# Fetching the second output tile's weights before the first's, in every pair of a block-product up-projection

## The chip, the cores and the metric

The kernel runs on one core of one Trainium2 chip. The metric is the time of one execution on the device, in microseconds (us), as the median of several runs. The core has a matrix engine (TensorE, PE in the profile), three engines that work on rows of data (VectorE, DVE; ScalarE, ACT; GpSimd, POOL), and SyncE (SP), which here issues the DMAs. Each engine works through its own queue of instructions in order and waits on semaphores for the others.

## The reference

The program is a small encoder of two layers with width 1024, all in 32-bit floats. Two sequences, a sample of 512 tokens and a prompt of 256, go through the same weights: 768 tokens in all. Layer 0 mixes tokens with an mLSTM, layer 1 with sliding-window attention. After the mixer, each layer has the part in which the change lies, a feed-forward network with a convolution of width 3 along the tokens:

```python
D_FF = 2816
def conv_ffn(h, w_up, conv_w, conv_b, w_down):
    u = h @ w_up                                  # [.., 1024] @ [1024, 2*2816]
    u = lax.conv_general_dilated(u, conv_w[:, None, :], window_strides=(1,),
                                 padding=((1, 1),), ...,
                                 feature_group_count=2 * D_FF) + conv_b
    g = u[..., :D_FF]
    val = u[..., D_FF:]
    return (jax.nn.silu(g) * val) @ w_down
...
x = x + g2 * conv_ffn(h, ffn_w_up[l], ffn_conv_w[l], ffn_conv_b[l], ffn_w_down[l])
```

## The kernel before

**Products in three parts.** TensorE multiplies a rounded 32-bit format (fp32r). To keep the accuracy of 32 bits, each operand is split in a rounded part hi and a remainder lo, and a product is hi·hi + hi·lo + lo·hi: three matmuls. `fp_copy_split` (L218 to L226) makes the two: ScalarE copies and rounds (L222, a CAST in the profile), VectorE subtracts (L223).

**Weights.** `load(u, h)` (L234) fetches one tile of 128 x 1024 floats (512 KB), half h of weight unit u, into one of five buffers named raw, with a DMA that SP issues (L231). All weights use this ring, those of the down-projection too, and the DMAs keep the order of the calls. `split` (L237) makes whi and wlo of a raw tile, with three buffers each.

**Rounds and pairs.** `ffn` (L1117) works through 11 rounds p = 0 to 10 in each layer. A round makes two pairs of output tiles of the up-projection: pair 0 gives 256 rows of the gate g, pair 1 the 256 rows of val that go with them. A pair is one weight unit: its two raw tiles are the weights of its first and of its second 128 rows of output, over all 1024 input channels. After the pairs of round p comes the down-projection of round p-1 (`down`), 96 matmuls on PSUM tiles named pa, with weights from two more raw tiles; L507 adds its results to the residual.

**A pair is a block product with seven multiplications instead of eight** (Strassen's scheme in Winograd's form). The weights are four blocks: A11 and A12 are the halves (512 columns) of the first tile `ra`, A21 and A22 those of the second tile `rb`; the code calls them q[0] to q[3]. The input, 8 x 128 channels by two halves of 384 tokens, is held as the blocks B11, B21, B22 and their combinations T1 to T4, split once per layer. Each of the seven products is `quarters` (L1034 to L1043): 12 matmuls of 128 x 128 by 128 x 384, at lines 1040, 1041 and 1042. The sums of the weight blocks overwrite the raw tiles in place:

- L1053: S1 = A21 + A22, into q[2]. It needs `rb` alone.
- The split of `ra` as fetched (wa) gives the weights of B11 and B21.
- L1055: S2 = S1 - A11 into q[0], after that split has read A11. L1056: S4 = A12 - S2 into q[1].
- L1078: S1 is split into s1h and s1l, one buffer each, for the product with T1.
- L1079: S3 = A22 - S2 into q[2], after S1 was split.
- The split of `ra` as it is now, S2 and S4 (wc), gives the weights of T2 and B22; the split of `rb`, S3 and A22 (wb), those of T3 and T4.

GpSimd makes these sums, but VectorE makes them for both pairs of round 0 and for pair 0 of round 1 (argument `pool_adds`).

**The PSUM banks of a pair.** Four banks are fixed: a takes B11 (later B21 on top of it), e takes T1, b starts as a copy of a and takes T2, d starts as a copy of b and takes T3 and T4; B22 goes on top of b. ScalarE makes these copies: L1086 (a to b), L1089 (e to p5, in SBUF), L1093 (b to d), L1107 (d to u3). T3 cannot start before the copy at L1093, and that copy not before T2's last matmul. The results go to SBUF by L1067 (ScalarE) and, with an addition, by L1112 and its neighbours (VectorE).

**After a pair**, each of its two rows goes through the convolution: L1127 (ScalarE), then two taps on VectorE, L1129 and L1130. A row of the gate goes through the silu (L1163, ScalarE). A row of val is multiplied with the gate's (L1165, GpSimd) and split.

**Round 0** is special: its two pairs are interleaved with the mixer's output projection and the normalisation of the tokens, whose pieces VectorE does too.

**Order of the work.** The order in which Python calls the operations is not the order in which the engines run them. The program is built with `schedule_with_timeline_sim=True`: a planner runs the whole program through a model of the chip's costs and orders each engine's queue by it. Where a tile becomes ready earlier or later in that model, it may order the queues around it differently.

Of the kernel before, what the change touches and what calls it, by code (L numbers as in the profile page):

```python
# [74 lines left out]
def col(t):  # L75

    return t + (GAP if t >= 256 else 0)


def pieces(c0, c1):  # L80

    return [(max(c0, s0), min(c1, s1), q) for q, (s0, s1) in enumerate(SEQS) if max(c0, s0) < min(c1, s1)]
# [55 lines left out]
class Net:  # L138
# [906 lines left out]
    def pair(self, pool, u, bank, rows, early=False, spare=False, pool_adds=True):  # L1045


        nc = self.nc
        r1, r2 = rows
        ra, rb = (self.load(u, h) for h in range(2))  # L1050
        q = [t[:, 512 * i : 512 * (i + 1)] for t in (ra, rb) for i in range(2)]
        tt = (nc.gpsimd if pool_adds else nc.vector).tensor_tensor
        tt(q[2], q[2], q[3], ALU.add)  # L1053
        wa = self.split(ra)
        tt(q[0], q[2], q[0], ALU.subtract)  # L1055
        tt(q[1], q[1], q[0], ALU.subtract)  # L1056
        if spare:
            s1h, s1l = (lambda t: (t[:, 0], t[:, 1]))(self.slab([P, 2, 512], R))
        else:
            s1h = pool.tile([P, 512], R, tag="s1h", name=self.nm("s1h"), bufs=1)  # L1060
            s1l = pool.tile([P, 512], R, tag="s1l", name=self.nm("s1l"), bufs=1)
        yield
        part = lambda w, i: [t[:, 512 * i : 512 * (i + 1)] for t in w]

        def evict(r, o):
            for p0, p1, _ in pieces(0, H):
                nc.scalar.copy(r[:, col(p0) : col(p0) + p1 - p0], o[:, p0:p1])  # L1067

        a = bank(0)
        self.quarters(a, part(wa, 0), self.B11, True)  # L1070
        fork = a
        if early:
            fork = self.tmp([P, H])
            nc.scalar.copy(fork, a)
            self.quarters(a, part(wa, 1), self.B21, False)
            evict(r1, a)
        yield
        self.fp_copy_split(s1h, s1l, q[2])  # L1078
        tt(q[2], q[3], q[0], ALU.subtract)  # L1079
        wc = self.split(ra)  # L1080
        if early:
            yield
        else:
            wb = self.split(rb)
        e, b = bank(1), bank(2)
        nc.scalar.copy(b, fork)  # L1086
        self.quarters(e, (s1h, s1l), self.T1, True)
        p5 = self.tmp([P, H])
        nc.scalar.copy(p5, e)  # L1089
        yield  # L1090
        self.quarters(b, part(wc, 0), self.T2, False)
        d = bank(3)
        nc.scalar.copy(d, b)  # L1093
        if early:
            wb = self.split(rb)
        yield
        p3 = lambda: self.quarters(b, part(wc, 1), self.B22, False)
        if early:
            p3()
            nc.vector.tensor_tensor(r1[:, col(H) :], b, p5, ALU.add)  # L1100
            yield
        else:
            self.quarters(a, part(wa, 1), self.B21, False)
            evict(r1, a)
        self.quarters(d, part(wb, 0), self.T3, False)
        u3 = self.tmp([P, H])
        nc.scalar.copy(u3, d)  # L1107
        yield
        if not early:
            p3()  # L1110
            nc.vector.tensor_tensor(r1[:, col(H) :], b, p5, ALU.add)
        nc.vector.tensor_tensor(r2[:, col(H) :], e, u3, ALU.add)  # L1112
        self.quarters(d, part(wb, 1), self.T4, False)
        evict(r2, d)
# [282 lines left out]
```

## Time and profile before

| | us |
|---|---|
| median of 3 runs | 1946.82 (1946.59 to 1949.53) |
| profiled execution | 1955.06 |
| its span, first to last instruction | 1953.2 |
| TensorE busy in the span | 1851.3 (95%) |
| VectorE busy | 1390.8 (71%) |
| ScalarE busy | 895.8 (46%) |
| GpSimd busy | 555.1 (28%) |

In the profile, a line of a group or of a timeline names the source line (L1053 is line 1053 of the kernel), the engine, the operation, and the tiles written and read. Brackets at the end of a timeline row give the idle time of that engine just before it, and what ended that wait. Matmuls are pipelined: each is listed with 0.34 us or so, but they start 0.175 us apart where nothing holds them up. The mean clock granted to TensorE over the span was 0.979 of full speed; it is lower in some stretches. The feed-forward network of layer 0 lies from about 545 to 1100 us, that of layer 1 from about 1386 to 1920 us; in between its rounds take about 47.6 us each.

### The profile page before, as it was taken

Reading aid. Unit: us, or ns where it says so; the run is one execution under the profiler, and the core shown is the slowest. Engines: PE = TensorE matmul, PEld = TensorE weight load, DVE = VectorE, ACT = ScalarE, POOL = GpSimd, SP = SyncE. Lnnn points to the kernel's source line nnn. Section 1 sums busy time; section 2 is a strip of 40 time slices with the busy share of each in tenths; the row PEclk is TensorE's granted clock in tenths of the full one; section 3 lists DMA queues with packets and bytes.
Section 4 is the critical chain, followed back from the end, with each engine's and each line's share of the span. In section 5 each row is a group of like instructions: output and inputs, shape, how many; then the busy total and the mean of one; then the engine's idle time right before and its main releaser. Section 6 shows DMA issues by size and latency. Waiting matters only on the chain. (4 is left out here: it accounts for less than half of the span.)

```text
span 1953.2 us, 28783 instructions
## 1 busy us (share of the span) xinstructions
PE 1851.3 (95%) x11122; PEld 1673.9 (86%) x11122; DVE 1390.8 (71%) x2261; ACT 895.8 (46%) x1785; POOL 555.1 (28%) x448
## 2 busy tenths in 40 slices
PE   6799999999979999999999999999799999999997
PEld 3686887888978999999999998779789999999997
DVE  4756675684577777777777765775877777777776
ACT  3343433343446444444444555774554444444442
POOL 4203011032213333333331311342123333333323
PEclk8899999999989999999999999999899999999998
DMA  9335445455212222222222221122212222222211
GB/s 341 100 100 188 150 155 198 150 157 169 76 44 76 65 66 65 65 65 65 65 66 87 98 89 49 40 85 76 65 56 65 72 69 66 72 68 65 65 33 66
DMA packets 63381, 181.32 MB, mean 93 GB/s; under 512 B 6071, under 2 KB 23735, under 8 KB 63244
## 3 DMA queue, kind: packets, MB, share of 16 engines
q1 hardware_dynamic: 63244, 179.49, 28.7%
q8 instruction: 87, 1.43, 0.3%
q14 instruction: 50, 0.41, 0.1%
HBM read 173.03 MB, written 6.43 MB: 92 GB/s over the span
## 5 line engine op out<-in xcount | busy, mean ns | idle before, releaser
L222 ACT CAST whi<-raw 128x1024 fp32r<-128x1024 f32 x247 | 258.5, 1047 | 414.0 <-PE pa L216 202.8
L223 DVE TENSOR_TENSOR wlo<-raw,whi 128x1024 fp32r<-128x1024 f32 x247 | 330.5, 1339 | 104.1 <-ACT whi L222 103.5
L216 PE MATMUL pa<-slab,whi 128*128 128x256 f32 (+1 forms) x1472 | 349.1, 335 | 3.7 <-DVE slab L507 2.6
L216 PEld LDWEIGHTS pa<-slab,whi 128*128 128x128 f32 x1472 | 253.4, 191 | 35.3 <-DVE slab L507 9.2
L507 DVE SCALAR_TENSOR_TENSOR slab<-pa,mod,slab 128x256 f32<-128x256 f32 (+1 forms) x368 | 206.9, 591 | 59.2 <-PE pa L216 59.1
L216 PE MATMUL pa<-slab,wlo 128*128 128x256 f32 (+1 forms) x736 | 234.6, 332 | 0.0
L216 PE MATMUL ps<-zh,whi 128*128 128x256 f32 (+2 forms) x688 | 230.1, 338 | 4.6 <-ACT zh L222 2.7
L216 PE MATMUL ps<-zh,wlo 128*128 128x256 f32 (+2 forms) x688 | 229.3, 337 | 2.8 <-DVE wlo L223 2.8
L216 PE MATMUL ps<-zl,whi 128*128 128x256 f32 (+2 forms) x688 | 231.0, 338 | 0.9 <-DVE zl L477 0.7
L1040 PE MATMUL ps<-zh,whi 128*128 128x384 f32 x504 | 173.7, 345 | 20.9 <-ACT ps L1093 18.2
L1041 PE MATMUL ps<-zl,whi 128*128 128x384 f32 x504 | 171.8, 341 | 4.1 <-DVE zl L223 4.1
L1042 PE MATMUL ps<-zh,wlo 128*128 128x384 f32 x504 | 171.5, 340 | 0.0
L216 PEld LDWEIGHTS pa<-slab,wlo 128*128 128x128 f32 x736 | 140.1, 191 | 12.3
L216 PEld LDWEIGHTS ps<-zh,whi 128*128 128x128 f32 x688 | 132.8, 194 | 20.2 <-ACT zh L222 3.5
L1053 POOL TENSOR_TENSOR raw<-raw 128x512 f32<-128x512 f32 x38 | 69.0, 1815 | 284.3 <-DMA raw<-in_w_dram 132.6
L216 PEld LDWEIGHTS ps<-zh,wlo 128*128 128x128 f32 x688 | 133.4, 194 | 14.1 <-DVE wlo L223 3.4
L216 PEld LDWEIGHTS ps<-zl,whi 128*128 128x128 f32 x688 | 133.4, 194 | 12.3 <-issue 1.7
L1130 DVE SCALAR_TENSOR_TENSOR slab<-slab,cstt,slab 128x771 f32<-128x771 f32 x88 | 131.5, 1496 | 1.4
L1165 POOL TENSOR_TENSOR slab<-slab 128x772 f32<-128x772 f32 x44 | 89.5, 2035 | 139.6 <-DVE slab L1130 124.8
L1055 POOL TENSOR_TENSOR raw<-raw,raw 128x512 f32<-128x512 f32 x38 | 49.1, 1291 | 266.5 <-DVE wlo L223 245.8
L1129 DVE SCALAR_TENSOR_TENSOR slab<-slab,cstt,slab 128x771 f32<-128x771 f32 x88 | 103.0, 1172 | 29.8 <-ACT slab L1127 29.8
L1040 PEld LDWEIGHTS ps<-zh,whi 128*128 128x128 f32 x504 | 96.2, 191 | 29.9 <-ACT ps L1093 24.0
(261 smaller groups left out, 4220.1 us busy)
## 6 DMA issues: line engine op xcount, KB each, us to landing
raw<-in_w_dram SPq DMA_DIRECT2D x202, 512.0 KB, 3.7
raw<-in_adaln_w_dram SPq DMA_DIRECT2D x84, 512.0 KB, 4.3
slab<-in_x_dram SPq DMA_DIRECT2D x12, 512.0 KB, 9.1
slab<-in_adaln_w_dram SPq DMA_DIRECT2D x12, 512.0 KB, 10.2
slab<-mrows SPq DMA_DIRECT2D x8, 384.0 KB, 4.8
xs<-slab SPq DMA_DIRECT2D x6, 512.0 KB, 2.9
bt<-brow SPq DMA_DIRECT2D x16, 192.0 KB, 3.2
slab<-xs SPq DMA_DIRECT2D x6, 512.0 KB, 9.3
```

Source lines behind the costliest of these rows:

```text
L216: self.nc.tensor.matmul(out, lhsT, rhs, start=start, stop=stop)
L222: nc.scalar.copy(hi, src)
L223: nc.vector.tensor_tensor(lo, src, hi.bitcast(F32), ALU.subtract)
L507: self.nc.vector.scalar_tensor_tensor(x, o, self.mod[l][:, gc + c, q : q + 1], x, ALU.mult, ALU.add)
L1040: mm(o, wh[:, k], hi[k], start=start and k == 0, stop=False, skip_group_check=True)
L1041: mm(o, wh[:, k], lo[k], start=False, stop=False, skip_group_check=True)
L1042: mm(o, wl[:, k], hi[k], start=False, stop=k == 3, skip_group_check=True)
L1053: tt(q[2], q[2], q[3], ALU.add)
L1055: tt(q[0], q[2], q[0], ALU.subtract)
L1129: stt(y[:, 1:], u[:, :-1], w(0), y[:, 1:], ALU.mult, ALU.add)
L1130: stt(y[:, :-1], u[:, 1:], w(2), y[:, :-1], ALU.mult, ALU.add)
L1165: nc.gpsimd.tensor_tensor(y, y, yrow[:, j], ALU.mult)
```

## The change

In each pair the two calls of `load` are made in the other order: the DMA of the second tile `rb` is now issued first, that of the first tile `ra` second. Names, sums, splits and products stay as they are. The lines after the changed one read the same tiles as before.

```diff
     def pair(self, pool, u, bank, rows, early=False, spare=False, pool_adds=True):
...
         nc = self.nc
         r1, r2 = rows
-        ra, rb = (self.load(u, h) for h in range(2))
+        rb, ra = (self.load(u, h) for h in (1, 0))
         q = [t[:, 512 * i : 512 * (i + 1)] for t in (ra, rb) for i in range(2)]
         tt = (nc.gpsimd if pool_adds else nc.vector).tensor_tensor
         tt(q[2], q[2], q[3], ALU.add)
```

It holds for all 44 pairs, in both layers, those of round 0 too. The planner builds the queues anew for the changed program.

## The prediction

> **What bounds the kernel now.** I read the page first, then the waits of the stretches in which the changed lines run, then the timeline of one pair of output tiles, engine by engine.
>
> ```profile
> PE 1851.3 (95%) x11122; PEld 1673.9 (86%) x11122; DVE 1390.8 (71%) x2261; ACT 895.8 (46%) x1785; POOL 555.1 (28%) x448
> ```
>
> TensorE is busy for 1851.3 of 1953.2 us. The change adds and removes no matmul, so only the 102 us in which TensorE stands still, and the clock it gets after standing still, can move. The list of waits over the whole span has two links of one chain:
>
> ```profile
> ACT s1h L222 <- POOL raw L1053: 53.3, 18, 3.5
> ...
> PE ps L1040 <- ACT ps L1093: 18.4, 19, 3.2
> ```
>
> Eighteen times the cast of S1 (s1h) waits on ScalarE for POOL's sum at L1053, and about as often (19) TensorE waits for the copy at L1093: 18.4 us in all. How they hang together is seen in one pair, the second pair of a round p from 3 to 9; here the one around 711 us. The columns are start, duration, engine, line, operation, tiles, and in brackets the idle time before and what ended it.
>
> ```profile
> 700.66 0.33 SPq L231 DMA_DIRECT2D raw<-in_w_dram  x1
> ...
> 709.90 0.33 SPq L231 DMA_DIRECT2D raw<-in_w_dram  x1
> ```
> ```profile
> 702.95 1.29 POOL L1055 TENSOR_TENSOR raw<-raw,raw 128x512 f32<-128x512 f32 x1 [13.59 <-DVE wlo L223]
> 704.31 1.29 POOL L1056 TENSOR_TENSOR raw<-raw 128x512 f32<-128x512 f32 x1
> 705.56 2.01 POOL L1079 TENSOR_TENSOR raw<-raw,raw 128x512 f32<-128x512 f32 x1
> 713.77 1.28 POOL L1053 TENSOR_TENSOR raw<-raw 128x512 f32<-128x512 f32 x1 [6.20 <-DMA raw<-in_w_dram]
> ```
> ```profile
> 709.24 1.03 ACT L222 CAST whi<-raw 128x1024 fp32r<-128x1024 f32 x1
> 710.17 0.53 ACT L1067 COPY slab<-ps 128x128 f32<-128x128 f32 x2
> 710.74 1.04 ACT L1127 ACTIVATE slab<-slab,cstt 128x772 f32<-128x772 f32 x1
> 711.68 0.46 ACT L1089 COPY nt<-ps 128x384 f32<-128x384 f32 x1
> 715.08 0.62 ACT L222 CAST s1h<-raw 128x512 fp32r<-128x512 f32 x1 [2.95 <-POOL raw L1053]
> 715.61 0.47 ACT L1093 COPY ps<-ps 128x384 f32<-128x384 f32 x1
> 716.02 0.84 ACT L1163 ACTIVATE slab<-slab 128x772 f32<-128x772 f32 x1
> ```
> ```profile
> 714.72 0.34 PE L1040 MATMUL ps<-yh,whi 128*128 128x384 f32 x1
> 714.89 0.34 PE L1041 MATMUL ps<-yl,whi 128*128 128x384 f32 x1
> 715.07 0.34 PE L1042 MATMUL ps<-yh,wlo 128*128 128x384 f32 x1
> 716.13 0.44 PE L1040 MATMUL ps<-zh,whi 128*128 128x384 f32 x1 [0.72 <-ACT ps L1093]
> ```
>
> Matmuls start 0.175 us apart, so product T3 could start at 715.24; it starts at 716.13, 0.89 us late. The copy it waits for (L1093) had its input early, but stands on ScalarE behind s1h; s1h stands behind POOL's L1053, and L1053 behind a DMA that was issued only at 709.90. That DMA is the raw tile rb of the next round's first pair. The tile loaded just ahead of it, ra, was issued at 700.66 and is not read before the split of the next round. Here the change takes hold: the two places in the DMA queue are swapped.
>
> **The change part by part.** It adds no instruction. SP issues the same DMAs in the same order and number; in each pair the first place now fetches the second tile's weights. The five raw slots come free in the same order, since the roles move with the tiles. Three things follow.
>
> *The first tile arrives later.* Its split now depends on the issue at 709.90, whose data were there 3.87 us later (713.77 less 709.90). The split of ra is this row:
>
> ```profile
> 725.11 1.06 ACT L222 CAST whi<-raw 128x1024 fp32r<-128x1024 f32 x1 [2.65 <-PE ps L1041]
> ```
>
> It starts 11.3 us after that and waits for a buffer, not for the data: cost nothing. If that cover were gone, TensorE would wait for ra with the whole product B11.
>
> *Rounds 3 to 9 of each layer, second pair: 14 pairs.* The planner that orders the queues moves the work. In the built program POOL's queue now has L1055, then L1053 of the next round's rb, then L1056 and L1079. ScalarE has L1127, s1h, L1089, the silu (L1163), and only then L1093: the copy loses one thing ahead of it, the late DMA, and gets another, the silu. VectorE has the S1 remainder (s1l) between the two taps L1129 and L1130. TensorE has five B21 matmuls before T2, five within, and two after it, where eight stood after it before. So T2's last matmul starts at 714.72, two matmuls ahead of T3's place, and only 0.35 us of other work covers the copy.
>
> ```profile
> 704.90 1.51 DVE L1129 SCALAR_TENSOR_TENSOR slab<-slab,cstt,slab 128x771 f32<-128x771 f32 x1 [1.17 <-ACT slab L1127]
> 706.34 0.55 DVE L1112 TENSOR_TENSOR slab<-ps,nt 128x384 f32<-128x384 f32 x1
> 706.81 1.58 DVE L1130 SCALAR_TENSOR_TENSOR slab<-slab,cstt,slab 128x771 f32<-128x771 f32 x1
> 708.31 1.21 DVE L223 TENSOR_TENSOR wlo<-raw,whi 128x1024 fp32r<-128x1024 f32 x1
> 710.30 1.23 DVE L223 TENSOR_TENSOR wlo<-raw,whi 128x1024 fp32r<-128x1024 f32 x1 [0.78 <-ACT whi L222]
> 711.81 1.02 DVE L1129 SCALAR_TENSOR_TENSOR slab<-slab,cstt,slab 128x771 f32<-128x771 f32 x1 [0.28 <-ACT slab L1127]
> 712.87 1.02 DVE L1130 SCALAR_TENSOR_TENSOR slab<-slab,cstt,slab 128x771 f32<-128x771 f32 x1
> 715.73 0.69 DVE L223 TENSOR_TENSOR s1l<-raw,s1h 128x512 fp32r<-128x512 f32 x1 [1.84 <-ACT s1h L222]
> ```
>
> These rows also show what it costs to put L1053 there. A tap takes 1.02 us by itself and 1.51 or 1.58 where it meets a POOL operation; L1079 takes 2.01 where it meets taps, L1056 1.29. The ends fit one operation at a time: L1129 ends 0.82 us after L1056, L1079 1.15 us after that L1129, L1130 0.82 us after L1079. L1112, which reads PSUM, runs through.
>
> The Trainium skill says the same ("SBUF — State Buffer", section "Who interferes with whom"): an exclusive lock between VectorE with two SBUF inputs and POOL, held for the whole instruction. By that rule and these rows the pair costs 0.19 us more; if they could run side by side T3 would come at 715.87, and the 14 pairs would save 3.6 us instead.
>
> With those steps: the DMA issued at 700.66 lands near 704.5 (plus 3.87). L1053 704.50 to 705.78; L1129 waits for it, to 706.61; L1056 to 707.76; L1130 to 708.58; L1079 to 709.73, that is 2.16 us later than now. The split of the T3 weights, now at 709.24, waits for L1079 and starts at 709.76: 0.52 late. L1067, L1127 and the second row's L1129 follow it on their queues, each 0.5 late: L1129 ends at 713.35. Then s1l 0.69, L1130 1.02 (to 715.02), silu 0.84 (to 715.90), the copy 0.47 with the overlap of 0.1 that queued ACT rows show (to 716.27). T3 starts at 716.32 against 716.13: 0.19 us later, times 14 is plus 2.7 us. Ends: if the copy could follow T2 at once (715.06 plus 0.47 and two handovers of 0.04), T3 would start at 715.62, minus 0.51 each, minus 7.1 us; if POOL and VectorE meet worse, the first rival below.
>
> *Round 1, second pair, once in each layer.* Here the same chain is longest.
>
> ```profile
> 601.20 4.91 POOL L1165 TENSOR_TENSOR slab<-slab 128x772 f32<-128x772 f32 x1 [5.32 <-ACT slab L1163]
> 606.07 1.29 POOL L1055 TENSOR_TENSOR raw<-raw,raw 128x512 f32<-128x512 f32 x1
> ...
> 616.51 2.06 POOL L1053 TENSOR_TENSOR raw<-raw 128x512 f32<-128x512 f32 x1 [5.92 <-DVE slab L1129]
> ```
> ```profile
> 616.16 0.34 PE L1042 MATMUL ps<-yh,wlo 128*128 128x384 f32 x1
> 619.66 0.45 PE L1040 MATMUL ps<-zh,whi 128*128 128x384 f32 x1 [3.16 <-ACT ps L1093]
> ```
> ```profile
> 612.00:624.00 12.00, 8.84 (x42) 8.52 (x41) 6.83 (x8) 6.72 (x13) 2.06 (x1) 0.86 0.35 96
> ```
>
> T3 comes 3.33 us late (619.66 less 616.33). The last row is a stretch of 12 us: the clock granted in it is 0.86 on average, a loss of 0.14 times 12, about 1.6 us. So this pair loses 4.9 us. In the new order 24 matmuls of the down projection stand between T2 and T3, 5.6 us of work at 0.23 us each (estimated from 512 against 384 columns), so the copy is covered. What is late next is their weights: the split of the down tile (whi) now stands behind s1h and L1089. L1053 takes L1055's place at 606.07 and pushes L1055, L1056 and L1079 by one operation (with the meetings, L1079 ends near 612.7); the T3 split 1.03 (to 613.7), L1067 0.53, silu 0.84, L1127 1.04, s1h 0.62, L1089 0.46 and the split 1.03, less overlaps of 0.1, end near 617.8. The 24 should start at 616.33, so they wait about 1.5 us, and some 0.4 more for the remainder wlo. I take 1.9 lost instead of 4.9, minus 3.0 a layer, minus 6.0 in all; ends: minus 4.9 each, and minus 0.4 each where the wait is 2.9 us and the clock is lost too.
>
> On the clock the Trainium skill has a rule that speaks against this term ("TensorE: Matmul & The Clock Gate", section "What's actually happening"): half rate only after an idle window of about 3.4 us, free-running. The stall of 3.16 us is shorter, and yet the clock fell, so here a stretch rather than a single gap seems to count. If stalls below a window cost nothing, the term would be 3.33 less 1.9, minus 1.4 a layer, and the whole sum minus 1.3 us instead of minus 4.5.
>
> *Round 2, second pair, once in each layer.*
>
> ```profile
> 668.56 0.44 PE L1040 MATMUL ps<-zh,whi 128*128 128x384 f32 x1 [0.62 <-ACT ps L1093]
> ```
>
> The new order puts twelve B21 matmuls (2.1 us) behind T2 where eight stood, so this wait should go: minus 0.6 each, minus 1.2; ends 0 and minus 0.8 each.
>
> *Round 0, once in each layer.* VectorE does the sums here, and is full.
>
> ```profile
> 545.12 0.45 PE L1040 MATMUL ps<-yh,whi 128*128 128x384 f32 x1 [1.25 <-DVE slab L507]
> ```
>
> L1053 and s1l of the first pair move ahead of the normalisation, one split remainder (1.21) moves behind it, and L1053 of round 1 moves ahead of the L507 that TensorE waits for. What leaves the queue ahead of that L507 is about what comes into it: taken as 0, ends minus 1.0 and plus 1.0 each.
>
> Sum: plus 2.7, minus 6.0, minus 1.2, 0: minus 4.5 us. The profiled execution took 1955.06 us (span 1953.2 and 1.86 around it), 8.2 us or 0.4% above the median of 1946.82; it would take 1950.6, and the median becomes 1942.3 us.
>
> **The rivals.** *POOL is starved (slower).* The place is L1079 of the 14 pairs. If the remainder wlo (1.21) gets in before L1079, because the T2 split is ready as L1130 ends, L1079 ends 1.2 us later, at 710.9, and everything to T3 with it: plus 1.36 a pair, 19.0 us in all, less 7.2 from the other terms: plus 11.8, 1958.6 us. For it: the 4.91 us row, a POOL operation kept out by three back-to-back VectorE ones. Against it: by the steps above the split ends at 708.85, 0.27 us after L1130, and POOL asks first. It decides from 0.51 us a pair (no gain left), and shows as slower from 0.79.
>
> *The wait only changes hands (no change).* In round 1 the down weights are so late that the clock falls again (minus 0.4 a layer), the pairs cost their 0.19, round 2 gains: plus 0.7 us, 1947.5. For it: every new order has the silu or a split ahead of the same copy.
>
> *The copy comes free (larger gain).* Minus 7.1 for the pairs, 9.8 for round 1, 1.2 for round 2: 18.1 us, 1928.7. Against it: silu and taps stand ahead of L1093 in the new queues.
>
> *The change does nothing*: the planner could have restored the old order of fetches. The built program speaks against it: rb is fetched first in every pair.
>
> **How the numbers follow.** Forecast 0.37, starved POOL 0.25, hands changed 0.25, copy free 0.10, nothing 0.03. 0.2% is 3.9 us, about what a measurement of this kernel can tell. The forecast lies just past it, so a quarter of its chance may fall inside; the small losses on either side of the third case go both ways. Faster 0.43, same 0.27, slower 0.30. The range goes from 1931 (most of the copy-free case) to 1958 (nearly all of the starved one, a pair that loses about 1.3 us); the forecast's own range is 1937 to 1948.
>
> **What would show it.** Right: no wait of s1h for L1053 and none of L1053 for a DMA of 6 us in rounds 3 to 9; POOL's order L1055, L1053, L1056, L1079; T3 still waiting for L1093, now right behind a silu, by 0.8 to 1.1 us against its place; no gap above 2.5 us near 620 and 1460. Wrong: T3 waits well below 0.5 us (copy free) or above 1.5 us (POOL starved), a wait before the down products in round 1 above 2.5 us with a granted clock below 0.9, or a new wait in round 0.

## The result, and the profile after

| | before | changed |
|---|---|---|
| median of 21 runs each | 1950.13 us | 1946.18 us |
| range | 1946.59 to 1955.12 | 1940.37 to 1951.58 |
| profiled execution | 1955.06 us | 1944.27 us |

The ratio is 0.9976, with a 95% interval from 0.9967 to 0.9985: faster by 0.24%, 4.7 us (the medians lie 3.95 us apart, the means 4.6). The three runs of before that were known ahead had a median of 1946.82; over 21 it is 1950.13.

The two profiled spans are 10.7 us apart, more than twice the effect. To compare parts, I take the start of the copy L1093 of each pair, which all traces show 44 times, as a clock mark: from the first mark of a layer to its last (the feed-forward network), the changed kernel takes 467.2 and 462.8 us where before took 468.0 and 468.8, so 6.8 us less. The other 3.9 us lie outside. There the order of ScalarE, VectorE and GpSimd is changed only in the first part of round 0, which lies ahead of the first mark, and one execution tells little: outside the networks the two profiles of the changed kernel themselves, 1942.5 and 1948.6 us long, differ by 6.6 us.

First the page's line of busy times, of the changed kernel, then two lines from its list of waits (total, times, longest).

```profile
PE 1844.8 (95%) x11122; PEld 1671.5 (86%) x11122; DVE 1381.2 (71%) x2261; ACT 894.4 (46%) x1785; POOL 555.6 (29%) x448
```
```profile
POOL raw L1053 <- DMA raw<-in_w_dram: 157.3, 28, 9.9
...
PE ps L1040 <- ACT ps L1093: 13.9, 16, 1.9
```

The 18 waits of s1h for L1053 are gone; TensorE still waits for L1093, 16 times, 13.9 us where it was 18.4. Round 1 is where it improved. The stretch of 12 us that had 8.84 us of TensorE work at a clock of 0.86, now:

```profile
612.00:624.00 12.00, 10.94 (x54) 9.19 (x53) 9.72 (x11) 6.65 (x12) 1.29 (x1) 1.00 0.41 131
```

TensorE's two waits in round 1, from the timeline:

```profile
617.03 2.10 PE L216 MATMUL pa<-slab,whi 128*128 128x512 f32 x8 [1.06 <-ACT whi L222]
...
645.06 0.50 PE L216 MATMUL pa<-slab,whi 128*128 128x256 f32 x2 [0.87 <-DVE slab L507]
```

The stall of 3.16 us became one of 1.06 us ahead of the down products and a new one of 0.87 us for a PSUM tile that L507 frees late. The clock stays at 1.00.

In rounds 3 to 9 the order is as it was read from the built queues. The second pair of round 5, layer 0:

```profile
794.01 1.29 POOL L1055 TENSOR_TENSOR raw<-raw,raw 128x512 f32<-128x512 f32 x1 [14.11 <-DVE wlo L223]
795.59 1.29 POOL L1053 TENSOR_TENSOR raw<-raw 128x512 f32<-128x512 f32 x1 [0.29 <-DMA raw<-in_w_dram]
796.83 2.02 POOL L1056 TENSOR_TENSOR raw<-raw 128x512 f32<-128x512 f32 x1
798.81 2.02 POOL L1079 TENSOR_TENSOR raw<-raw,raw 128x512 f32<-128x512 f32 x1
803.33 0.60 ACT L222 CAST s1h<-raw 128x512 fp32r<-128x512 f32 x1
806.10 0.85 ACT L1163 ACTIVATE slab<-slab 128x772 f32<-128x772 f32 x1 [1.80 <-DVE slab L1130]
806.86 0.47 ACT L1093 COPY ps<-ps 128x384 f32<-128x384 f32 x1
807.38 0.44 PE L1040 MATMUL ps<-zh,whi 128*128 128x384 f32 x1 [0.92 <-ACT ps L1093]
```

L1055 started at 702.95 in the pair of before and at 794.01 here, a shift of 91.06. In that frame L1079 ends at 709.77, L1093 at 716.27, and T3 starts at 716.32: the copy waits for the silu now, 0.19 us later than it did for the late sum.

What the prediction did not have is at the end of the same pair, where the second row goes through the taps. Before (round 5, layer 1):

```profile
1658.92 1.01 DVE L1129 SCALAR_TENSOR_TENSOR slab<-slab,cstt,slab 128x771 f32<-128x771 f32 x1
1659.17 1.91 POOL L1053 TENSOR_TENSOR raw<-raw 128x512 f32<-128x512 f32 x1 [7.89 <-DVE wlo L223]
1659.97 1.93 DVE L1130 SCALAR_TENSOR_TENSOR slab<-slab,cstt,slab 128x771 f32<-128x771 f32 x1
1662.05 1.85 POOL L1165 TENSOR_TENSOR slab<-slab 128x772 f32<-128x772 f32 x1 [0.97 <-DVE slab L1130]
1662.49 2.50 DVE L223 TENSOR_TENSOR wlo<-raw,whi 128x1024 fp32r<-128x1024 f32 x1
```

and the changed kernel at the same place:

```profile
1653.09 1.02 DVE L1129 SCALAR_TENSOR_TENSOR slab<-slab,cstt,slab 128x771 f32<-128x771 f32 x1
1654.14 1.02 DVE L1130 SCALAR_TENSOR_TENSOR slab<-slab,cstt,slab 128x771 f32<-128x771 f32 x1
1655.31 1.86 POOL L1165 TENSOR_TENSOR slab<-slab 128x772 f32<-128x772 f32 x1 [7.15 <-DVE slab L1130]
1656.62 1.63 DVE L223 TENSOR_TENSOR wlo<-raw,whi 128x1024 fp32r<-128x1024 f32 x1
```

There are two L1053 in a round: one for the next round's first pair, and a second one, for its second pair. Before, the second ran into L1130 (1.93 us instead of 1.02), which pushed L1165, and that the remainder wlo (2.50 instead of 1.63). Now this L1053 is done before the taps start. L507, which frees a PSUM tile, stands behind that remainder, and TensorE feels it some 9 us on; before (the first row is a weight load, PEld, which waits for L507):

```profile
1671.63 0.30 PEld L216 LDWEIGHTS pa<-slab,whi 128*128 128x128 f32 x2 [0.40 <-DVE slab L507]
1671.22 0.34 PE L1042 MATMUL ps<-zh,s1l 128*128 128x384 f32 x1
1671.63 0.73 PE L216 MATMUL pa<-slab,whi 128*128 128x512 f32 x2
1672.20 0.39 PE L216 MATMUL pa<-slab,wlo 128*128 128x512 f32 x1
```

and changed:

```profile
1665.38 0.34 PE L1042 MATMUL ps<-zh,s1l 128*128 128x384 f32 x1
1665.56 0.62 PE L216 MATMUL pa<-slab,whi 128*128 128x512 f32 x2
1666.02 0.39 PE L216 MATMUL pa<-slab,wlo 128*128 128x512 f32 x1
```

From the matmul at 1671.22 to that at 1672.20 it is 0.98 us before, and 0.64 between the same two now: 0.34 us a round. On the matmuls themselves the pieces are too short for the list of waits, but on the weight loads the list of before has them; first its line, then that of the kernel with second pairs only, from the next section:

```profile
PEld pa L216 <- DVE slab L507: 9.2, 21, 0.7
...
PEld pa L216 <- DVE slab L507: 2.4, 4, 0.7
```

Before, 14 of the 21 are at this one place, 0.35 to 0.41 us in every round from 3 to 9; in the changed kernel no weight load waits for L507 there.

### The profile page after: what moved, and what is told of

Read it like the earlier page. It is cut to its first block, busy times and chain, and to the rows that moved or that the text cites. A ratio compares the mean times of both kernels' runs of the same rounds, so it can differ in the third digit from the quotient of the medians.

```text
span 1942.5 us, 28786 instructions
## 1 busy us (share of the span) xinstructions
PE 1844.8 (95%) x11122; PEld 1671.5 (86%) x11122; DVE 1381.2 (71%) x2261; ACT 894.4 (46%) x1785; POOL 555.6 (29%) x448
## 4 chain that ended last, share of the span: by engine, by line
PE 71%; DVE 11%; issue 7%; POOL 5%; DMA 3%; ACT 2%; SPq 0%; POOLq 0%; DVEq 0%; ACTq 0%
PE pa L216 24%; PE ps L216 17%; PE ps L1040 9%; PE ps L1041 9%; PE ps L1042 9%; DVE wlo L223 3%; DMA raw<-in_w_dram 2%; PE pa L899 2%; DVE slab L507 1%; DMA slab<-in_adaln_w_dram 1%; POOL nt L106 1%; ACT whi L222 1%; POOL hs L734 1%; POOL slab L491 1%; DVE slab L1129 1%
## 5 line engine op out<-in xcount | busy, mean ns | idle before, releaser
L223 DVE TENSOR_TENSOR wlo<-raw,whi 128x1024 fp32r<-128x1024 f32 x247 | 336.1, 1362 | 114.3 <-ACT whi L222 113.2
L507 DVE SCALAR_TENSOR_TENSOR slab<-pa,mod,slab 128x256 f32<-128x256 f32 (+1 forms) x368 | 208.3, 591 | 75.6 <-PE pa L216 75.3
L1165 POOL TENSOR_TENSOR slab<-slab 128x772 f32<-128x772 f32 x44 | 89.9, 2043 | 248.6 <-DVE slab L1130 237.9
L216 PEld LDWEIGHTS ps<-zh,whi 128*128 128x128 f32 x688 | 132.6, 194 | 19.8 <-ACT zh L222 3.8
L216 PEld LDWEIGHTS ps<-zh,wlo 128*128 128x128 f32 x688 | 133.2, 194 | 13.9 <-DVE wlo L223 3.3
L1129 DVE SCALAR_TENSOR_TENSOR slab<-slab,cstt,slab 128x771 f32<-128x771 f32 x88 | 104.1, 1185 | 29.5 <-ACT slab L1127 29.2
L1055 POOL TENSOR_TENSOR raw<-raw,raw 128x512 f32<-128x512 f32 x38 | 50.6, 1331 | 246.8 <-DVE wlo L223 246.8
L1130 DVE SCALAR_TENSOR_TENSOR slab<-slab,cstt,slab 128x771 f32<-128x771 f32 x88 | 118.7, 1350 | 0.8
L1040 PE MATMUL ps<-yh,whi 128*128 128x384 f32 x336 | 114.5, 341 | 4.3 <-DVE slab L507 3.5
L433 DVE SCALAR_TENSOR_TENSOR ada<-raw,silc,ada 128x1024 f32<-128x1024 f32 x84 | 109.0, 1330 | 11.8 <-DMA raw<-in_adaln_w_dram 11.8
```

The costliest lines, as they stand in the source:

```text
L216: self.nc.tensor.matmul(out, lhsT, rhs, start=start, stop=stop)
L223: nc.vector.tensor_tensor(lo, src, hi.bitcast(F32), ALU.subtract)
L433: stt(acc[:, s], row, w, acc[:, s], ALU.mult, ALU.add)
L507: self.nc.vector.scalar_tensor_tensor(x, o, self.mod[l][:, gc + c, q : q + 1], x, ALU.mult, ALU.add)
L1040: mm(o, wh[:, k], hi[k], start=start and k == 0, stop=False, skip_group_check=True)
L1129: stt(y[:, 1:], u[:, :-1], w(0), y[:, 1:], ALU.mult, ALU.add)
```

## The experiments

Rounds are measured by the mark of the first pair's L1093, from one round to the next. The table has the median of the 14 rounds that start at rounds 3 to 9 of the two layers, the two rounds 1 and 2 together (98.00 and 98.18 us before), and the network's time in both layers, all of the one profiled execution; the ratio is that of the timed runs, beside before on the same chip. The changed kernel's second ratio would not clear the noise by itself; its interval overlaps the first.

| kernel | ratio, 95% | one round, 3 to 9 | rounds 1 and 2 | both networks |
|---|---|---|---|---|
| before | | 47.59 | 98.00, 98.18 | 936.9 |
| changed | 0.9976 (0.9967 to 0.9985) | 47.39 | 94.98, 95.00 | 930.1 |
| changed, again | 0.9984 (0.9967 to 1.0001) | 47.46 | 94.90, 95.19 | 929.5 |
| first pairs only | 0.9999 (0.9983 to 1.0016) | 47.85 | 95.66, 95.46 | 937.3 |
| second pairs only | 0.9960 (0.9943 to 0.9976) | 47.23 | 95.08, 97.38 | 928.4 |
| rounds 0 to 2 | 1.0005 (0.9987 to 1.0022) | 47.59 | 95.58, 95.64 | 930.4 |
| rounds 0 to 2, again | 1.0021 (1.0004 to 1.0037) | 47.59 | 95.62, 95.66 | 931.1 |
| rounds 3 to 10 | 0.9910 (0.9885 to 0.9935) | 46.44 | 97.61, 97.01 | 918.1 |
| rounds 1 to 10 | 0.9984 (0.9971 to 0.9997) | 47.39 | 95.11, 95.12 | 928.5 |
| pinned, all rounds | 0.9894 (0.9877 to 0.9911) | 46.24 | 93.12, 93.19 | 907.7 |
| pinned from round 3 | 0.9906 (0.9887 to 0.9924) | 46.24 | 94.56, 94.61 | 910.7 |
| pinned, first pairs only | 0.9922 (0.9903 to 0.9941) | 46.73 | 95.08, 94.75 | 917.7 |

**The two tiles apart.** After the two traces were compared, my theory was that all of it comes from rb of the first pairs, since the planner moves the queues for that tile alone. The rival: rb of the second pairs takes the collision with the taps away. The line in one kernel, with the remainder 1 in the condition for the other:

```diff
-        rb, ra = (self.load(u, h) for h in (1, 0))
+        rb, ra = (self.load(u, h) for h in (1, 0)) if (u - U_FFN) % 3 == 0 else [self.load(u, h) for h in (0, 1)][::-1]
```

> Only pair 0 of each round (the gate's rows) fetches its second tile first; pair 1 keeps the old order. My theory: what matters is the raw tile rb of the next round's first pair, so this kernel has the whole effect: built, it has the same TensorE queue as the changed kernel; ratio to before 0.9976 (0.996 to 0.999), a wait of about 1 us instead of 3.2 us in round 1, and in rounds 3 to 9 a round of 47.3 us instead of 47.6. Rival: the sum at L1053 whose collision with the convolution taps is gone in the changed kernel is that of pair 1, so the tile of pair 1 has to come earlier: then the taps at the end of pair 1 still take 1.9 us here, rounds stay at 47.6 us, and only round 1 gains: 0.9968 of before less nothing else, or 6 us.

> Only pair 1 of each round (val's rows) fetches its second tile first. My theory: no effect, ratio 1.000 (0.999 to 1.001); TensorE waits 0.72 us for L1093 in rounds 3 to 9 and 3.2 us in round 1 as before. Rival (the tile of pair 1 takes the collision away): rounds 3 to 9 0.3 us shorter each, 14 of them, 4.6 us, ratio 0.9976.

The rival was right and my theory fell. With first pairs only, built with the TensorE queue of the changed kernel, a round is longer than before, 47.85 us. The second L1053 is as late as ever and meets the taps, and the weight load that waited 0.40 us for L507 before waits about 0.53:

```profile
1750.99 1.88 POOL L1053 TENSOR_TENSOR raw<-raw 128x512 f32<-128x512 f32 x1 [12.48 <-DVE slab L1111]
1751.64 2.05 DVE L1129 SCALAR_TENSOR_TENSOR slab<-slab,cstt,slab 128x771 f32<-128x771 f32 x1
...
1755.33 2.51 DVE L223 TENSOR_TENSOR wlo<-raw,whi 128x1024 fp32r<-128x1024 f32 x1
```

With second pairs only, the queues of TensorE, ScalarE and POOL are built in the old order, and VectorE's but for one instruction moved in round 0 of each layer. Only the time at which a tile arrives differs, and that takes the collision away:

```profile
1645.81 1.72 POOL L1053 TENSOR_TENSOR raw<-raw 128x512 f32<-128x512 f32 x1 [0.81 <-DMA raw<-in_w_dram]
1646.07 0.44 PE L1040 MATMUL ps<-zh,whi 128*128 128x384 f32 x1 [0.72 <-ACT ps L1093]
...
1652.63 1.02 DVE L1129 SCALAR_TENSOR_TENSOR slab<-slab,cstt,slab 128x771 f32<-128x771 f32 x1
1653.68 1.02 DVE L1130 SCALAR_TENSOR_TENSOR slab<-slab,cstt,slab 128x771 f32<-128x771 f32 x1
```

T3 waits 0.72 us as ever; the round is 0.36 us shorter by the medians, 4.8 us in the sum of the 14. The rest of what its networks lose, 3.7 us, lies in rounds 1 and 2, most of it (2.9) in layer 0, where T3 waited 2.31 us in round 1 and the clock stayed at 1.00; in layer 1 it waited 3.16 us as before, with the clock at 0.88 over 14 us. Whether the shorter wait comes from the change was not tested.

**Rounds apart.** The condition on the same line became `(u - U_FFN) % (3 * NPART) < 9` for rounds 0 to 2, and `>= 9` for rounds 3 to 10.

> The new order of fetches in rounds 0 to 2 only. My theory: the stall of 3.2 us in round 1 and the clock lost behind it are gone, once in each layer, minus 3.1 us each: ratio 0.9968 (0.996 to 0.998); rounds 3 to 9 stay at 47.6 us with the wait of 0.72 us for L1093. Rival: the gain lies in the 14 pairs of rounds 3 to 9, then this kernel stands at 1.000 (0.999 to 1.001).

> The new order of fetches from round 3 on only. Round 1 keeps its stall of 3.2 us. Built, its steady rounds are planned another way than in the changed kernel: the copy L1093 stands ahead of the silu L1163, and four matmuls stand between T2 and T3. My theory says that in the changed kernel the silu ahead of L1093 is what TensorE waits for now (0.66 to 0.97 us) and that the collision of L1053 with the taps cost 0.33 us a round: without both, a round loses 0.72 plus 0.33 us, 14 of them, 14.7 us less some 2 for late DMAs: ratio 0.9935 (0.992 to 0.996). Rival: the copy is not held by the silu but by TensorE or the splits, and the rounds are as in the changed kernel, 47.3 us: 14 times 0.33, 0.9976.

Rounds 0 to 2: the trace shows what was expected (rounds 1 and 2 lose 2.4 and 2.5 us, the networks 6.4 in all), the time shows nothing, 1.0005. Rounds 3 to 10: 0.991, beyond the changed kernel itself. Here the planner put the copy ahead of the silu:

```profile
1688.67 0.46 ACT L1093 COPY ps<-ps 128x384 f32<-128x384 f32 x1
1690.33 0.85 ACT L1163 ACTIVATE slab<-slab 128x772 f32<-128x772 f32 x1 [1.19 <-DVE slab L1130]
```

No wait for L1093 of 0.3 us or more is left in rounds 3 to 9, and a round takes 46.44 us. That agrees with the silu as what holds the copy in the changed kernel: here it starts 1.66 us behind the copy's start, and the copy needs nothing from it. Other queues differ too, so it is not the only change.

**The changed kernel again, and without round 0.** (The condition `// 3 >= 1` on the same quantity.)

> The changed kernel once more, for a second profile beside the next three. Ratio 0.9976 (0.996 to 0.999). Rounds 6 and 8 of layer 0 had their copy 1.9 us late in the first profile, behind a POOL sum that waited 0.96 us for its data, and both had an instruction fetch in the same microseconds as that load. If the fetch is the cause (my theory), it comes at the same place of the program again: the same two rounds show 1.9 us. If it was chance (rival), other rounds or none do.

> All rounds but round 0 take the new order; built, the TensorE queue of rounds 1 to 10 is that of the changed kernel. Rounds 0 to 2 alone gave 1.0005 although their two stalls of 3.2 us went, minus 2.5 us a layer in its trace, so something gave 5 us back. My theory: round 0, where TensorE waits longer for L507 (1.44 and 2.08 us against 1.25 and 1.53) and the clock may fall behind the longer wait; without round 0 this kernel should beat the changed one: 0.9955 (0.994 to 0.997). Rival: round 0 does not matter, 0.9976, and the result of rounds 0 to 2 was scatter.

Rounds 6 and 8 of layer 0 wait 1.9 us again, in both the first and the second profile of the changed kernel; the first:

```profile
843.38 1.02 DVE L1129 SCALAR_TENSOR_TENSOR slab<-slab,cstt,slab 128x771 f32<-128x771 f32 x1 [1.16 <-ACT slab L1127]
843.68 1.88 POOL L1053 TENSOR_TENSOR raw<-raw 128x512 f32<-128x512 f32 x1 [0.96 <-DMA raw<-in_w_dram]
...
847.49 1.29 POOL L1079 TENSOR_TENSOR raw<-raw,raw 128x512 f32<-128x512 f32 x1
...
855.75 0.44 PE L1040 MATMUL ps<-zh,whi 128*128 128x384 f32 x1 [1.87 <-ACT ps L1093]
```

and the second:

```profile
856.14 0.44 PE L1040 MATMUL ps<-zh,whi 128*128 128x384 f32 x1 [1.88 <-ACT ps L1093]
952.06 0.45 PE L1040 MATMUL ps<-zh,whi 128*128 128x384 f32 x1 [1.87 <-ACT ps L1093]
```

The DMA view of the 5.6 us around that load, in the first profile (queue, packets, MB, share; then the time to landing):

```profile
q8 instruction: 1, 0.02, 1.4%
raw<-in_w_dram SPq DMA_DIRECT2D x1, 512.0 KB, 4.4
```

and the same lines for the load of round 5, from 791.5 to 795.8 us:

```profile
q8 instruction: 1, 0.02, 1.4%
raw<-in_w_dram SPq DMA_DIRECT2D x1, 512.0 KB, 3.7
```

In round 6 the load takes 4.4 us instead of 3.7. L1053 waits 0.96 us, VectorE's tap gets in first, and counted from L1055 the last sum, L1079, starts 1.3 us later than in round 5. What makes the load late stays open. My theory was the instruction fetch (queue q8) in the same microseconds, but a fetch falls into the load of round 5 as well, which takes 3.7 us. Nor are the two rounds fixed: in the kernel without round 0, round 6 waits 1.87 us again and round 8 only 0.75. Round 0 makes no difference that these runs can tell: 0.9984 with it and without.

**The sum's place in POOL's queue.** If the early tile is good and the sum ahead of L1056 and L1079 is not, the sum can be pinned to its old place:

```diff
-        tt(q[2], q[2], q[3], ALU.add)
+        with self.tc.issue_after(self.s3.ins) if self.s3 is not None else nullcontext(): tt(q[2], q[2], q[3], ALU.add)
...
-        tt(q[2], q[3], q[0], ALU.subtract)
+        s3 = tt(q[2], q[3], q[0], ALU.subtract); self.s3 = s3 if pool_adds and (u - U_FFN) % 3 == 1 else None
```

The first two kernels of this kind made S3 (L1079) only where another sum is pinned behind it; they left it out in all first pairs and in the second pair of round 0.

> The changed kernel, with one order pinned: L1053 of the next round's first pair is issued on POOL behind L1079 of this round's second pair, as in the kernel before. So the tile is early, but POOL's queue is the old one, and the late DMA no longer stands in front of L1056 and L1079. Built, ScalarE has the copy L1093 ahead of the silu. My theory: the wait for L1093 in rounds 3 to 9 (0.72 us) goes with the sum no longer late and no longer ahead of L1079, and the collision with the taps (0.36 us) stays gone: rounds of 46.5 us, 14 times 1.08 is 15.1 us, and rounds 1 and 2 gain 3 us a layer as in the changed kernel or more: 21 us, ratio 0.989 (0.987 to 0.991). Rival (what holds T3 is the row of splits on ScalarE, not the sum): rounds of 47.2 us, 0.996.

> The same pinned order, and round 0 left as in the kernel before. If round 0 costs (my theory): 1 to 5 us less than with all rounds, ratio 0.987 (0.985 to 0.989). If it does not (rival): the same as with all rounds.

They came to 0.9854 (0.9835 to 0.9874) and 0.9842 (0.9818 to 0.9866), with rounds of 46.24 us. With 24 sums missing they compute something else, and these ratios are not those of the order alone. So with every sum made (from round 3, the condition for the pin is `(u - U_FFN) % 3 == 1 and (u - U_FFN) % 33 >= 6`):

> The two runs named sum_behind left out the sum S3 at L1079 in the first pairs of the rounds, and in the second pair of round 0, so their times are not those of the pinned order alone. Here every sum is made, and only the order is pinned: L1053 of the next round's first pair is issued on POOL behind L1079 of this round's second pair, in all rounds. Built, POOL and TensorE have the old order in rounds 3 to 9, ScalarE has the copy L1093 ahead of the silu. My theory: with the old order of POOL the tile's early arrival is free: no wait for L1093, no collision, rounds of 46.5 us (46.2 to 46.8) instead of 47.6: 14 times 1.1 is 15.4 us; round 1 has the old TensorE order again and keeps most of its 3 us stall: ratio 0.992 (0.989 to 0.994). Rival: the 46.24 us of the sum_behind runs came from the sum that was left out, and rounds are as in the changed kernel, 47.2 to 47.4: 0.997.

> The same pin, but only for the sums of rounds 3 and later; rounds 0 to 2 keep the changed kernel's order. My theory adds the two parts: rounds 0 to 2 minus 3 us a layer, 14 rounds minus 1.1 us each, 21 us: ratio 0.989 (0.987 to 0.991), the fastest. Rival: rounds 0 to 2 give nothing that lasts, as their run alone showed (1.0005), then 0.992.

> As pinned_from_round_3, but only the first pairs fetch their second tile first. My theory: the two tiles have separate effects. The first pair's takes the wait of 0.72 us for L1093 away, the second pair's the collision of 0.36 us: here the wait goes and the collision stays, rounds of 46.9 us, 0.36 longer than with both: 0.9915. Rival: with the gate pair's sum out of the way the other L1053 comes earlier too and meets no tap, then rounds are as with both swaps, 46.5 us.

The rounds are 46.24 us with every sum as well, so what was left out had no part in that. T3's place in the pinned kernel:

```profile
792.53 2.02 POOL L1053 TENSOR_TENSOR raw<-raw 128x512 f32<-128x512 f32 x1
...
799.03 0.46 ACT L1093 COPY ps<-ps 128x384 f32<-128x384 f32 x1 [1.37 <-PE ps L1042]
799.46 0.85 ACT L1163 ACTIVATE slab<-slab 128x772 f32<-128x772 f32 x1
...
800.25 0.34 PE L1040 MATMUL ps<-zh,whi 128*128 128x384 f32 x1
```

The copy now waits for T2's last matmul (1.37 us), and T3 no longer waits for the copy: it starts with no gap. A round is 1.35 us shorter than before. With first pairs only it is 46.73: the first pair's tile is worth 0.86 us when its sum keeps its place, the second pair's 0.49 more. Whether rounds 0 to 2 are pinned too or keep the changed kernel's order made no clear difference (0.9894 against 0.9906, intervals overlapping); pinned in all rounds, 1926.95 us against 1948.96, is the fastest kernel here.

> The new order in rounds 0 to 2 only, once more, since the trace showed 6 us gone from rounds 1 to 3 of both layers and the time did not. My theory: scatter of the mixer part; this time 0.997 (0.995 to 0.999). Rival: something outside rounds 1 to 10 gives it back each time: 1.000 (0.999 to 1.002).

Again the networks lose 5.8 us in the trace, and the time is not less (1.0021). My theory, scatter, does not stand after two sets of 12 runs. The same holds in part elsewhere: the kernel pinned in all rounds loses 29.1 us in its networks and 20.7 in time (0.0106 of 1948.96), rounds 1 to 10 lose 8.4 and 3.1, pinned first pairs 19.2 and 15.2. In three kernels the two numbers agree: first pairs only (0.4 longer, 0.2 less), second pairs only (8.4 and 7.8), rounds 3 to 10 (18.8 and 17.6). So by these numbers 2 to 10 us come back outside the networks in the other kernels, each from one profile and a ratio that is good to 3 or 4 us. Most of these swap both pairs of rounds 1 and 2, but pinned first pairs do not. There is a lead: ahead of the first mark of layer 1, in round 0, TensorE waits for L507, 1.53 us before and 1.10 to 1.53 in the three kernels that agree, but 1.94 to 2.57 in six of the other eight profiles (1.66 and 1.34 in the kernels pinned from round 3 and pinned with first pairs only). The clock can fall behind such a wait, as the last section shows; in the first profile of rounds 0 to 2 it did in both layers, and the stretches from there to the first mark took 73.2 us together instead of 68.0. But in the kernel pinned in all rounds they took 68.0 as well, so this is not the whole of it, and what does it stays open.

## Why the prediction came out

The time was forecast at minus 4.5 us and came at minus 4.7 (as a median, 1942.3 against 1946.18, since before itself came out 3.3 us higher over 21 runs). That the two are so close is luck: the parts fit less well than the sum.

*Rounds 3 to 9, plus 0.19 us a pair.* The working holds within 0.04 us in round 5 of layer 0 (L1079's end predicted at 709.73, measured 709.77; T3 at 716.32 both). It does not hold alike in all pairs: in layer 1 T3 waits 0.66 to 0.84 us where before it waited 0.72. From a round's mark to T3 the 14 stretches grew by 2.65 us together, close to the 2.7 forecast, but 2.3 of it are the two late pairs of rounds 6 and 8; the median grew by 0.09. First pairs alone do not isolate it either: their rounds are longer (47.85 us against 47.59), but the stretch ahead of T3 grew by 0.04 us in the median and the one behind it, with the wait for L507, by 0.14.

*What the term left out.* The prediction says "in each pair the first place now fetches the second tile's weights", and I followed that to the next round's first pair only. The tile of the second pair, whose L1053 met the taps, was priced at nothing: 0.36 us a round, minus 4.8 us in 14. This is the step that failed, and it is as large as the forecast. The rows of the collision were there to be read before. One of the signs that were to show the forecast right fails with it: L1053 still waits for a DMA, 7.24 us in the round 5 shown (at 808.07), but it is now the sum of the second pair, whose tile arrives second.

*The starved POOL*, a rival with a chance of 0.25, happened in 2 of 14 pairs, at L1053 and not at L1079: my landing time of 3.87 us left the sum about 0.4 us of margin (L1053 at 704.50, the tap at 704.90 in the rows of before), and a load that took 4.4 us lost POOL its turn. T3 came 1.15 us later than in before there (1.87 against 0.72), where I had priced the rival at 1.36.

*Round 1, minus 3.0, round 2, minus 0.6 a layer.* Together minus 3.6; measured minus 3.0 and 3.2. Only the sum can be compared: by the marks round 1 is 3.6 us shorter and round 2 is 0.5 us longer, and the new queues can put other matmuls between the same marks. The wait ahead of the down products was forecast at 1.5 plus 0.4, and is 1.06; the clock stayed up as forecast; the wait of 0.87 us for L507 was not foreseen. Round 2's wait is gone as forecast.

*Round 0, zero within 1 us.* Within its ends in the waits: those for L507 grew from 1.25 and 1.53 to 1.52 and 1.94 us, and leaving round 0 out changed nothing that the ratios show. The clock behind these waits is part of the open point.

The sum of the 14 rounds is minus 0.6 us in the first profile and minus 1.3 in the second, against plus 2.7 forecast; with rounds 1 and 2 the networks lose 6.8 and 7.4. In the first profile, minus 4.5 was forecast, the missing term adds minus 4.8, a clock that fell in round 8 of layer 0 cost 1.5, and rounds 1 and 2 gained 1.0 less than forecast: minus 6.8. That the time shows 4.7 is part of the open point above. So the sign was right, and the size came out because a missing term was made up for by losses that were not foreseen either.

On the rule of the Trainium skill about the shared lock ("SBUF — State Buffer", "Who interferes with whom"), the collisions shown above agree: a tap takes 1.02 us alone and 1.93 to 2.05 where L1053 is under way. On its rule of the clock ("TensorE: Matmul & The Clock Gate", "What's actually happening") the last section has numbers.

## What to carry to other kernels

When the order of loads changes, follow every tile that it moves to its first reader, and look there at what that reader stands next to on the shared resource; the gain in rounds 3 to 9 came from a sum that no longer met the taps, and of that the list of waits shows only 0.4 us at a time, on the weight loads. An operation that becomes ready earlier is not always better placed earlier: the planner let a sum for the next round pass two that the present product needed, and with that sum pinned behind them the same change is worth 1.06% instead of 0.24%. Where the margin between landing and use is about 0.4 us, as here, some rounds can miss it: two of 14 did.

## What the runs showed that I had not expected

The clock behind the same wait differs from one execution to another. In round 0 of layer 1 TensorE waits 1.53 us for L507 and then works through the same 59 or 60 matmuls. The windows (length, TensorE busy, weight loads, VectorE, ScalarE, POOL, granted clock, DMA share, GB/s) of before, and of the kernel with rounds 3 to 10:

```profile
1385.50:1396.00 10.50, 9.56 (x60) 9.24 (x61) 5.72 (x10) 4.45 (x9) 0.86 (x1) 1.00 0.17 50
```
```profile
1378.00:1393.00 15.00, 14.16 (x59) 13.84 (x60) 5.63 (x10) 4.44 (x9) 1.25 (x1) 0.66 0.11 35
```

9.56 us at a clock of 1.00 in one, 14.16 us at 0.66 in the other. So the clock behind one such wait costs 4.6 us or nothing. In the same way, the 6 us behind the wait of 1.88 us in round 8 of the changed kernel, first profile:

```profile
951.60:957.60 6.00, 6.00 (x25) 6.00 (x26) 1.78 (x2) 1.98 (x5) 2.30 (x1) 0.72 0.29 89
```

and behind the 1.87 us at the same place in the second:

```profile
952.10:958.10 6.00, 6.00 (x32) 5.68 (x33) 3.94 (x4) 3.50 (x6) 1.30 (x1) 1.00 0.26 77
```

25 matmuls at a clock of 0.72 against 32 at 1.00. The Trainium skill ("TensorE: Matmul & The Clock Gate", "What's actually happening") puts the fall of the clock behind an idle window of about 3.4 us that runs freely; that the outcome varies for the same wait agrees with a free-running window, but waits of 1.53 and 1.88 us were enough here.
